# Gate and up of the second FFN by a seven-product (Strassen-Winograd) identity, with the down products of the previous tile set between them

## The chip, the cores and the metric

One core of one Trainium2 chip runs the whole program in one launch. The metric is the device time in microseconds (us), the median of several executions.

## The reference, cut to what matters

One layer of a diffusion backbone over 1024 latent tokens of width 1024 and 256 context tokens. Only its last part is touched by the change:

```python
def swiglu(h, w_gu, w_down):
    gate, up = jnp.split(h @ w_gu, 2, axis=-1)
    return (jax.nn.silu(gate) * up) @ w_down
...
x = x + mx[5] * mix_x
x = x + 0.5 * mx[8] * swiglu(modulate(x, g_ffn2[l], mx[6], mx[7]), w_gu2[l], w_down2[l])
...
return rmsnorm(x, g_final)
```

Here `h` is 1024 x 1024, `w_gu` 1024 x 5632 and `w_down` 2816 x 1024, all float32.

## The kernel before

Every matrix product is made of three matmuls (`mm3`, lines 622 to 626): both operands are split into a rounded high part H and a rest L, and H·H, H·L and L·H are summed in one PSUM bank. A split (`split`, line 618) is a copy on ScalarE (line 619, it writes H) and a subtraction (line 62, it writes L) on GpSimd (POOL) or VectorE (DVE).

`mix_out_ffn2` is the last part of the program. Its first half, the output projection, goes over eight token tiles `t` of 128 tokens. `part(t, ...)` issues 48 matmuls into two banks named `wo`; `evac(t)` scales them, adds them to the residual stream `acc[t]`, and takes the sum of squares; `xnorm(t)` writes the normalised tile `xn`. For odd t, `z_T` (line 1600) transposes the next two tiles of `z` after k = 4 of `part(t)`; DVE scales them just before. The first tile of gate and up weights is loaded (`w2r`) and split here, at t = 2 to 5. At t = 6 `trans(0, k)` transposes and modulates tokens 0 to 511 into `hT[0]` (H and L, eight k tiles).

The second half calls `ffn` (line 656). The hidden width is cut into NF = 22 tiles `f` of 128. For one f, gate is [128 hidden, 512 tokens], a sum over eight k tiles, for two token blocks b; up is the same. That is 4 results x 8 k x 3 = 96 matmuls of 512 columns, in banks `gu`. The down product adds, for each of eight token tiles and two halves of the 1024 outputs, one `mm3` into a bank `dn`, which DVE adds to `acc`: 16 x 3 = 48 matmuls for one f. The order on TensorE (PE) is gate(f), all down tiles of f-1, up(f). For f = 0 the transposes of tokens 512 to 1023 are set between the matmuls of block 1. The last two f (20 and 21, `joint`) are summed in one bank per down tile, and each finished token tile is normalised and stored while the next is computed (`final`). Weights stream in by DMA, 512 KB a piece, into four `raw` buffers, and are split on arrival; the down weight is first multiplied by the gate row `g8` on DVE (`raw<-raw,g`).

Each engine works through its own list in order, and waits on semaphores where the next instruction's data or buffer is not ready.

Of the kernel before, what the change touches and what calls it, by code (L numbers as in the profile page):

```python
# [15 lines left out]
MUL, ADD, SUB, POW = ALU.mult, ALU.add, ALU.subtract, ALU.pow  # L16

D = 1024
KT = 8
NX = 8  # L20
# [3 lines left out]
NF = FF // 128  # L24
# [23 lines left out]
class Kernel:  # L48
    def __init__(self, tc, a, out, dbg=None):
        self.tc, self.nc, self.a, self.out = tc, tc.nc, a, out  # L50
        self.dbg = dbg or {}
# [566 lines left out]
    def split(self, raw, H, L, eng=None):  # L618
        self.nc.scalar.activation(out=H, in_=raw, func=AF.Copy)  # L619
        self.tt(L, raw, H.bitcast(F32), SUB, eng)  # L620
# [953 lines left out]
    def mix_out_ffn2(self, sbig):  # L1574
        nc, a, acc = self.nc, self.a, self.acc
        B2 = [(0, 4), (4, 4)]
        with ExitStack() as st:
            hA = self.pool(st, "hT2a")
            hT = [tuple(hA.tile([128, KT, 512], F32R, name=f"h{x}0") for x in "HL")]
            w2 = self.pool(st, "w2")  # L1580
            P = {"w": w2}
            xp = self.pool(st, "xn", bufs=4)
            with ExitStack() as s1:
                tp = self.pool(s1, "wo", bufs=2)
                sm = self.pool(s1, "wos")
# [61 lines left out]
                def evac(t):  # L1647
                    ps = PS.pop(t)
                    for half in range(2):
                        cs = slice(half * 512, half * 512 + 512)  # L1650
                        self.stt(mo[:, cs], ps[half], ra[:, t:t + 1], g5[:, cs], MUL, MUL)
                    self.tt(acc[t], acc[t], mo, ADD, nc.gpsimd)
                    R[t] = self.rstd(self.sumsq(acc[t], mo, "n"), D, "n")

                def xnorm(t):
# [20 lines left out]
                def trans(b, kt, tag="gu"):  # L1676
                    self.modT([XN[i] for i in range(4 * b, 4 * b + 4)], kt, 2, 0, tag, hT[b], hf)
# [16 lines left out]
                    if t % 2 and k == 4 and t < NX - 1:  # L1694
                        z_T(t // 2 + 1)

                pre0 = {}
                for t in range(2, NX):
                    if t in (2, 4):
                        which = t // 2 - 1  # L1700
                        wr = sm.tile([128, D], F32, tag="wor", name="w2r")
                        nc.sync.dma_start(wr, a["w_gu2"][0, which].rearrange("p k f -> p (k f)"))
                    if t in (3, 5):
                        pre0[0, which] = [tuple(w2.tile([128, 1024], F32R, tag=f"w{x}{which}", name=f"w{x}{which}")
                                                for x in "HL")]
                        self.split(wr, *pre0[0, which][0], nc.gpsimd)
                    part(t, range(8), lambda k: pre(t, k))
                    if t % 2:
                        nxt(t // 2 + 1)
                    evac(t)  # L1710
                    for i in {2: (1,), 3: (2,), 4: (3,), 6: (4, 5), 7: (6, 7)}.get(t, ()):
                        xnorm(i)
                sbig.close()
                hB = self.pool(st, "hT2b", side="right")
                hT.append(tuple(hB.tile([128, KT, 512], F32R, name=f"h{x}1") for x in "HL"))
            P["act"] = P["wd"] = self.pool(st, "act2", bufs=2)
            P["raw"] = self.pool(st, "raw2", bufs=4)
            P["sg"], P["nsg"] = self.pool(st, "sg2"), 3
            fin = self.pool(st, "fin2")
            g8 = fin.tile([128, D], F32, name="g8")  # L1720
            gf = fin.tile([128, D], F32, name="gf")
            self.gate_bc(g8, (8, 0))
            nc.sync.dma_start(gf, a["g_final"].to_broadcast([128, D]))
            P["gates"] = [(g8, P["act"])]
            out = self.out.rearrange("(j s) d -> j s d", s=NX)

            def hook(b):
                todo = list(range(KT if b else 0))

                def pre(kt):  # L1730
                    while todo and todo[0] <= kt + 2:
                        trans(1, todo.pop(0), "dn")
                return pre

            down = self.ffn(B2, hT, a["w_gu2"], a["w_down2"], acc, P, hook, preload=pre0, keep=True, joint=True)
            S = {}

            def post(t, cs, p):
                self.tt(acc[t][:, cs], p, acc[t][:, cs], ADD)

            def final(t):
                R = self.rstd(S.pop(t), D, "n")
                for q in range(2 if t == NX - 1 else 1):
                    cs = slice(q * 512, q * 512 + 512) if t == NX - 1 else slice(0, D)
                    self.stt(J[t][:, cs], acc[t][:, cs], R, gf[:, cs], MUL, MUL)
                    nc.sync.dma_start(out[:, t, cs], J[t][:, cs])

            J = {}
            for t in range(NX):
                down([t], post)  # L1750
                J[t] = xp.tile([128, D], F32, tag="xn", name="j")
                S[t] = self.sumsq(acc[t], J[t], "n")
                if t:
                    final(t - 1)
            final(NX - 1)


def layouts(inp):
# [76 lines left out]
```

## Time and profile before

| | |
|---|---|
| median of 3 runs | 2529.99 us (2527.86 to 2538.18) |
| the profiled execution, its own time | 2531.55 us |
| its span | 2529.8 us, 31981 instructions |
| PE busy | 2417.6 us (96%), 12100 matmuls |
| DVE, ACT, POOL busy | 1454.1 (57%), 819.8 (32%), 1041.7 (41%) |

The span runs from the first to the last instruction; 1.75 us of the execution's own time lie around it. A busy share is the part of the span in which the engine ran an instruction. Matmuls are pipelined, so that one takes 0.39 us from its start to its end, but the next one starts earlier.

### The profile page before, as it was taken

How to read it: one execution, taken by the hardware profiler on the slowest of the kernel's cores; microseconds unless marked ns; L12 is line 12 of the kernel's file. 1: busy time of each engine (PE TensorE's matmuls, PEld its weight loads, DVE VectorE, ACT ScalarE, POOL GpSimd, SP SyncE). 2: the span in 40 equal slices, each digit the busy share in tenths (PEclk: the TensorE clock that was granted, in tenths of full speed). 3: DMA queues.
4: the chain of work that ended last, by engine and by line, in shares of the span. 5: the costliest groups of instructions: out<-in, count | busy, mean ns of one | idle time of the engine just before them, and what ended most of it. 6: DMA issues, size and time to landing. Idle time of an engine off the chain costs nothing. (4 is left out here: it accounts for less than half of the span.)

```text
span 2529.8 us, 31981 instructions
## 1 busy us (share of the span) xinstructions
PE 2417.6 (96%) x12100; PEld 1999.2 (79%) x12100; DVE 1454.1 (57%) x2468; ACT 819.8 (32%) x1572; POOL 1041.7 (41%) x949
## 2 busy tenths in 40 slices
PE   7999999999999998988999999999999999999998
PEld 3788888888888887887787777777788888888886
DVE  3666466966554627647788888862344444444443
ACT  4311211121111111633777777762411111111112
POOL 2422321254344334525676666755433322332222
PEclk9999999999999999999999999999999999999999
DMA  7232352122222232415000000123211111111111
GB/s 282 77 108 93 125 175 84 47 63 65 76 84 76 64 97 95 138 46 184 23 17 4 14 14 25 40 91 99 75 51 50 43 50 50 51 50 42 50 42 67
DMA packets 83544, 185.14 MB, mean 73 GB/s; under 512 B 22199, under 2 KB 41911, under 8 KB 82366
## 3 DMA queue, kind: packets, MB, share of 16 engines
q1 hardware_dynamic: 59990, 163.93, 19.4%
q10 hardware_dynamic: 23400, 19.16, 2.6%
q8 instruction: 95, 1.56, 0.2%
q14 instruction: 59, 0.48, 0.1%
HBM read 155.52 MB, written 27.54 MB: 72 GB/s over the span
## 5 line engine op out<-in xcount | busy, mean ns | idle before, releaser
L62 POOL TENSOR_TENSOR wL<-raw,wH 128x1024 fp32r<-128x1024 f32 x130 | 316.3, 2437 | 767.6 <-ACT wH L619 749.6
L62 DVE TENSOR_TENSOR acc<-dn,acc 128x512 f32<-128x512 f32 x540 | 366.9, 690 | 338.8 <-PE dn L626 338.6
L624 PE MATMUL gu<-big,wH 128*128 128x512 f32 (+1 forms) x1056 | 379.7, 360 | 4.9 <-ACT wH L619 2.3
L626 PE MATMUL gu<-big,wL 128*128 128x512 f32 (+1 forms) x1056 | 374.8, 355 | 4.6 <-POOL wL L62 4.6
L625 PE MATMUL gu<-big,wH 128*128 128x512 f32 (+1 forms) x1056 | 374.7, 355 | 1.8 <-POOL big L62 1.8
L624 PE MATMUL dn<-wH,aH 128*128 128x512 f32 x792 | 313.5, 396 | 10.7 <-DVE acc L62 5.5
L625 PE MATMUL dn<-wL,aH 128*128 128x512 f32 x792 | 310.5, 392 | 1.7 <-POOL wL L62 1.7
L626 PE MATMUL dn<-wH,aL 128*128 128x512 f32 x792 | 310.4, 392 | 1.1 <-POOL aL L62 1.1
L62 DVE TENSOR_TENSOR sg<-gu,sg 128x512 f32<-128x512 f32 (+1 forms) x110 | 69.9, 636 | 376.7 <-PE gu L626 348.8
L625 PE MATMUL gu<-hL,wH 128*128 128x512 f32 x704 | 274.6, 390 | 4.2 <-POOL hL L62 3.0
L619 ACT ACTIVATE wH<-raw 128x1024 fp32r<-128x1024 f32 x130 | 136.3, 1056 | 436.2 <-DVE raw L62 227.7
L624 PE MATMUL gu<-hH,wH 128*128 128x512 f32 x704 | 274.6, 390 | 0.0
L626 PE MATMUL gu<-hH,wL 128*128 128x512 f32 x704 | 274.0, 389 | 0.0
L62 POOL TENSOR_TENSOR aL<-sg,aH 128x512 fp32r<-128x512 f32 (+1 forms) x110 | 139.0, 1264 | 296.9 <-ACT aH L619 296.5
L624 PEld LDWEIGHTS gu<-big,wH 128*128 128x128 f32 x1056 | 200.0, 189 | 37.3 <-issue 3.3
L626 PEld LDWEIGHTS gu<-big,wL 128*128 128x128 f32 x1056 | 199.9, 189 | 34.4 <-POOL wL L62 6.4
L625 PEld LDWEIGHTS gu<-big,wH 128*128 128x128 f32 x1056 | 200.1, 190 | 31.1 <-POOL big L62 2.2
L619 ACT ACTIVATE aH<-sg 128x512 fp32r<-128x512 f32 (+1 forms) x110 | 64.5, 588 | 473.4 <-DVE sg L62 458.9
L62 DVE TENSOR_TENSOR ptL<-pt,ptH 128x512 fp32r<-128x512 f32 x240 | 162.7, 685 | 52.2 <-ACT ptH L1427 51.6
L624 PEld LDWEIGHTS dn<-wH,aH 128*128 128x128 f32 x792 | 150.1, 190 | 43.7 <-DVE acc L62 6.7
L625 PEld LDWEIGHTS dn<-wL,aH 128*128 128x128 f32 x792 | 150.1, 190 | 33.7 <-POOL wL L62 2.3
L626 PEld LDWEIGHTS dn<-wH,aL 128*128 128x128 f32 x792 | 149.8, 189 | 33.2 <-POOL aL L62 1.6
(318 smaller groups left out, 4635.2 us busy)
## 6 DMA issues: line engine op xcount, KB each, us to landing
raw<-in_w_gu SPq DMA_DIRECT2D x86, 512.0 KB, 3.4
wmr<-in_w_mod SPq DMA_DIRECT2D x56, 512.0 KB, 4.0
raw<-in_w_down SPq DMA_DIRECT2D x44, 512.0 KB, 4.7
row<-d_s SPq DMA_DIRECT2D x16, 576.0 KB, 3.7
wm<-in_w_mod SPq DMA_DIRECT2D x8, 1024.0 KB, 9.4
d_s<-T ACTq DMA_DIRECT2D x32, 160.0 KB, 2.7
ck<-d_s SPq DMA_DIRECT2D x16, 320.0 KB, 3.8
acc<-in_x SPq DMA_DIRECT2D x8, 512.0 KB, 9.1
```

Source lines behind the costliest of these rows:

```text
L62: (eng or self.nc.vector).tensor_tensor(out=out, in0=a, in1=b, op=op)
L619: self.nc.scalar.activation(out=H, in_=raw, func=AF.Copy)
L624: mm(out, lhsT=AH, rhs=BH, start=start, stop=False)
L625: mm(out, lhsT=AH, rhs=BL, start=False, stop=False)
L626: mm(out, lhsT=AL, rhs=BH, start=False, stop=stop)
```

## The change

With A11, A12 = the two k halves of the gate weight, A21, A22 = those of the up weight, B11, B21 = the k halves of tokens 0 to 511, and B12, B22 = those of tokens 512 to 1023, gate and up for both blocks are a 2 x 2 block product, which takes eight half products. The change computes it with seven:

- sums of weights, for each f: S1 = A21 + A22, S2 = S1 - A11, S3 = A11 - A21, S4 = A12 - S2 (DVE, `Products.add`; for f = 0 `Products.sums`, which uses one tile `s` for S1, S2 and S4 in turn);
- sums of tokens, once: T1 = B12 - B11, T2 = B22 - T1, T3 = B22 - B12, T4 = B21 - T2 (`part` in `ffn2`). B11 and B21 exist only as H and L; PE adds them up with a rounded identity `one` into banks `rc`;
- seven products of four k tiles each, 12 matmuls a product: A11·B11, S2·T2, S3·T3, S1·T1, A12·B21, A22·T4, S4·B22. DVE and ACT combine the banks in four 512-wide pieces of `acc[8]` and `acc[9]` (`P1`, `U2`, `U3`, `C22`), and the two activations of one f come out one after the other.

Each operand is split into H and L on ACT and POOL, seven splits of 128 x 512 for one f. The down products of f-1 are issued two token tiles at a time between the products of f. The down tiles of f = 20 are no longer joined to those of f = 21. There is one raw buffer for each weight half and one for the down weight. The last `acc` add of the output projection goes from POOL to DVE.

```diff
-                    self.tt(acc[t], acc[t], mo, ADD, nc.gpsimd)
+                    self.tt(acc[t], acc[t], mo, ADD, None if t == NX - 1 else nc.gpsimd)
...
                 for t in range(2, NX):
-                    if t in (2, 4):
-                        which = t // 2 - 1
-                        wr = sm.tile([128, D], F32, tag="wor", name="w2r")
-                        nc.sync.dma_start(wr, a["w_gu2"][0, which].rearrange("p k f -> p (k f)"))
-                    if t in (3, 5):
...
-                        self.split(wr, *pre0[0, which][0], nc.gpsimd)
+                    if t == 2:
+                        wr = [sm.tile([128, D], F32, tag="wor", name="w2r"), raw1.tile([128, D], F32, tag="r", name="w2r")]
+                        for which in range(2):
+                            nc.sync.dma_start(wr[which], a["w_gu2"][0, which].rearrange("p k f -> p (k f)"))
+                    if t == 3:
+                        prep = ops.sums(*wr, xp.tile([128, 512], F32, tag="hf", name="s", bufs=2))
+                    if t in (3, 4, 5):
+                        next(prep, None)
                     part(t, range(8), lambda k: pre(t, k))
...
-            down = self.ffn(B2, hT, a["w_gu2"], a["w_down2"], acc, P, hook, preload=pre0, keep=True, joint=True)
...
+    def ffn2(self, st, sx, h0, ops, raw1, xp, XN):
...
+        def part(k, tt, one):
+            f, r = [], []
+            for kt, pool, tag in ((k, xp, "hf"), (k + 4, tt, "b22")):
+                t = self.bank("dn", "tp")
+                for i in range(4):
+                    nc.tensor.transpose(t[:, i * 128:(i + 1) * 128], XN[4 + i][:, kt * 128:(kt + 1) * 128], self.ident)
+                x = pool.tile([128, 512], F32, tag=tag, name=tag, bufs=2)
+                nc.scalar.activation(out=x, in_=t, func=AF.Identity, scale=av[:, kt:kt + 1], bias=bv[:, kt:kt + 1])
+                f.append(x)
+            for x in ("B11", "B21"):
+                p = self.bank("dn", "rc")
+                for i in range(2):
+                    nc.tensor.matmul(p, lhsT=one, rhs=B[x][i][:, k, :], start=(i == 0), stop=(i == 1))
+                r.append(p)
...
+            self.tt(t1, b12, r[0], SUB)
+            self.split(t1, *g("T1"), nc.gpsimd)
+            self.tt(t2, b22, t1, SUB)
+            self.split(t2, *g("T2"), nc.gpsimd)
+            self.tt(t4, r[1], t2, SUB)
+            self.tt(t3, b22, b12, SUB)
+            self.split(t4, *g("T4"))
+            self.split(t3, *g("T3"), nc.gpsimd)
+            self.split(b22, *g("B22"), nc.gpsimd)
...
+                sx.close()
...
+                self.gate_bc(g8, (8, 0))
+                load_gu(1, (1,))
+                fetch_wd(0)
+                ops.add(*W[1], temps)
+                for x in ("S2", "S3", "S1"):
+                    ops.split(x)
+                load_wd(0)
+            else:
+                more = f + 1 < NF
+                fetch_wd(f)
+                nc.scalar.copy(P1, whole("A11"))
...
+                self.tt(U2, whole("S2"), P1, ADD)
...
+                down(f - 1, (0, 1))
+                self.tt(U3, whole("S3"), U2, ADD)
+                if more:
+                    ops.add(*W[f + 1], temps)
+                down(f - 1, (2, 3))
+                p = whole("S1")
+                self.tt(C22, p, U3, ADD)
+                self.tt(U2, p, U2, ADD)
+                for x in ("A11", "S2", "S3", "S1") if more else ():
+                    ops.split(x)
+                if f > 1:
+                    self.tt(P1, whole("A12"), P1, ADD)
+                    nc.scalar.activation(out=P1, in_=P1, func=AF.Silu)
+                down(f - 1, (4, 5))
+                p4 = whole("A22")
+            self.tt(U3, p4, U3, ADD)
+            self.tt(P1, P1, U3, MUL)
+            act[f] = [split_act(0, P1)]
+            if f:
+                down(f - 1, (6, 7))
+                load_wd(f)
+            self.tt(U2, whole("S4"), U2, ADD)
+            nc.scalar.activation(out=U2, in_=U2, func=AF.Silu)
+            self.tt(C22, U2, C22, MUL)
+            act[f].append(split_act(1, C22))
+            if f + 1 < NF:
+                for x in ("A12", "A22", "S4")[f == 0:]:
+                    ops.split(x)
+            load_gu(f + 2)
...
+            R, J = self.rstd(S.pop(t), D, "n"), acc[8 + t % 2]
...
+    def sums(self, g, u, t):
...
+        k.tt(t, a21, s["A22"], ADD)
+        s["S1"] = s["S2"] = s["S4"] = t
+        self.split("S1")
+        k.tt(t, t, s["A11"], SUB)
+        self.split("S2")
+        yield
```

`load_wd(f)` multiplies the down weight by `g8` on DVE and splits it on ACT and POOL, as before. `whole(x)` issues one product of 12 matmuls.

Three places show how instructions moved. First, DVE at t = 3 of the output projection, where `z<-z,ia` is the scaling ahead of `z_T` and `s` and `w2r` are the tile for the sums and the raw weight:

```order
 L66 TENSOR_SCALAR rv<-ss 128x1
 L66 TENSOR_SCALAR xn<-acc,rr 128x1024
+L62 TENSOR_TENSOR s<-w2r 128x512
+L62 TENSOR_TENSOR s<-s,w2r 128x512
 L66 TENSOR_SCALAR z<-z,ia 128x256 x2
 L62 TENSOR_TENSOR big<-zt,big 128x256 x2
```

S1 and S2 now stand ahead of the scaling of z, and the second of them overwrites the tile that the first wrote.

Second, DVE in the first step (f = 0) of the changed kernel, one of four quarters k; `hf` and `b_...` are b12 and b22, `rc` a PSUM bank, `t_...` T1, T2, T4 and T3 in this order:

```order
L62 TENSOR_TENSOR t_16534<-hf,rc 128x512
L62 TENSOR_TENSOR t_16535<-b_16526,t_16534 128x512
L62 TENSOR_TENSOR t_16537<-rc,t_16535 128x512
L62 TENSOR_TENSOR t_16536<-b_16526,hf 128x512
L62 TENSOR_TENSOR T4L<-t_16537,T4H 128x512
```

Before, DVE had one subtraction `hL<-hf,hH` for every second k tile there; now it has five operations for each pair of k tiles, three of them (T2, T3 and T4L) with both inputs in SBUF.

Third, DVE in one f of the steady part, before and then changed (`S_...` and `A_...` are banks of products, `rw` a raw weight, `wdr` the raw down weight):

```order
L62 TENSOR_TENSOR acc<-dn,acc 128x512 x16
L62 TENSOR_TENSOR raw<-raw,g_16405 128x1024
L62 TENSOR_TENSOR sg<-gu,sg 128x512 x2
```

```order
L62 TENSOR_TENSOR s<-rw,s 128x512
L62 TENSOR_TENSOR acc<-dn,acc 128x512 x4
L62 TENSOR_TENSOR acc<-S_17325,acc 128x512 x2
L62 TENSOR_TENSOR acc<-A_17356,acc 128x512
L62 TENSOR_TENSOR acc<-dn,acc 128x512 x4
L62 TENSOR_TENSOR acc<-A_17391,acc 128x512
L62 TENSOR_TENSOR acc<-acc 128x512
L62 TENSOR_TENSOR acc<-dn,acc 128x512 x4
L62 TENSOR_TENSOR wdr<-wdr,g_16692 128x1024
L62 TENSOR_TENSOR acc<-S_17435,acc 128x512
```

The multiplication of the down weight by `g8` used to stand ahead of up(f), with the 96 matmuls of up(f) and gate(f+1) between it and the down tiles that need it; now it stands behind the adds of the last two down tiles of f-1, and only the 36 matmuls of S4·B22, A11·B11 and S2·T2 come before the next down tiles.

## Rows read from the trace of the kernel before

**Rows 1.** The page, part 4: the chain that ended last, by line.

```profile
PE gu L625 6%; PE gu L626 6%; PE gu L624 6%; PE dn L626 3%; PE dn L625 3%; PE dn L624 3%; DVE acc L62 0%; DVE j L69 0%; POOL rr L62 0%; DVEq L1828 0%; POOLq L1828 0%; DVE rv L66 0%; POOLq L62 0%
```

**Rows 2.** Windows: us, busy of PE, PEld, DVE, ACT, POOL, PE clock, DMA share, GB/s.

```profile
1900.00:2000.00 100.00, 100.00 (x443) 82.81 (x442) 42.30 (x61) 16.28 (x22) 31.10 (x16) 1.00 0.14 48
```

**Rows 3.** Timeline of PE: start, us, operation; second FFN's first matmul, two in between, first last-step down.

```profile
1790.73 0.39 PE L624 MATMUL gu<-hH,wH 128*128 128x512 f32 x1
...
1849.93 0.39 PE L624 MATMUL gu<-hH,wH 128*128 128x512 f32 x1
...
1862.17 0.39 PE L624 MATMUL gu<-hH,wH 128*128 128x512 f32 x1
...
2496.61 0.39 PE L624 MATMUL dn<-wH,aH 128*128 128x512 f32 x1
```

**Rows 4.** Groups by line and shape, 1850 to 2490 us: busy us, mean ns, idle before.

```profile
L62 DVE TENSOR_TENSOR acc<-dn,acc 128x512 f32<-128x512 f32 x304 | 206.9, 692 | 204.8 <-PE dn L626 204.8
L62 DVE TENSOR_TENSOR raw<-raw,g 128x1024 f32<-128x1024 f32 x20 | 24.3, 1217 | 0.0
L62 POOL TENSOR_TENSOR wL<-raw,wH 128x1024 fp32r<-128x1024 f32 x59 | 141.5, 2398 | 333.6 <-ACT wH L619 333.6
L62 POOL TENSOR_TENSOR aL<-sg,aH 128x512 fp32r<-128x512 f32 x40 | 51.7, 1294 | 114.7 <-ACT aH L619 114.7
L619 ACT ACTIVATE wH<-raw 128x1024 fp32r<-128x1024 f32 x59 | 62.1, 1052 | 211.5 <-DVE raw L62 211.5
L619 ACT ACTIVATE aH<-sg 128x512 fp32r<-128x512 f32 x40 | 25.3, 632 | 162.8 <-DVE sg L62 162.8
```

**Rows 5.** Timeline of DVE and POOL: subtractions with two SBUF inputs, adds from PSUM.

```profile
1772.37 0.69 DVE L62 TENSOR_TENSOR hL<-hf,hH 128x512 fp32r<-128x512 f32 x1 [1.18 <-ACT hf L614]
...
1776.57 1.30 POOL L62 TENSOR_TENSOR hL<-hf,hH 128x512 fp32r<-128x512 f32 x1 [1.35 <-DVE hf L66]
1776.62 1.80 DVE L62 TENSOR_TENSOR hL<-hf,hH 128x512 fp32r<-128x512 f32 x1
...
2062.97 10.21 DVE L62 TENSOR_TENSOR acc<-dn,acc 128x512 f32<-128x512 f32 x15
...
2063.35 2.41 POOL L62 TENSOR_TENSOR wL<-raw,wH 128x1024 fp32r<-128x1024 f32 x1 [7.47 <-ACT wH L619]
```

**Rows 6.** Timeline of PE in the first step (f = 0): first and last wait, one transpose.

```profile
1804.37 0.50 PE L625 MATMUL gu<-hL,wH 128*128 128x512 f32 x1 [0.56 <-DVE hL L62]
...
1807.13 0.60 PE L607 MATMUL tp<-ident,xn 128*128 128x128 f32 x4
...
1815.99 0.50 PE L625 MATMUL gu<-hL,wH 128*128 128x512 f32 x1 [0.95 <-POOL hL L62]
```

**Rows 7.** Timeline of DVE and PE around `z_T` at t = 3.

```profile
1737.05 0.61 DVE L66 TENSOR_SCALAR z<-z,ia 128x256 f32<-128x256 f32 x2
...
1738.42 0.60 PE L1600 MATMUL zt<-ident,z 128*128 128x128 f32 x4
```

**Rows 8.** DMA issues, 1790 to 1800 us, then out from 1800 us: KB, us to landing.

```profile
raw<-in_w_gu SPq DMA_DIRECT2D x3, 512.0 KB, 7.0
gf<-in_g_final SPq DMA_DIRECT2D x1, 512.0 KB, 5.1
...
out<-j SPq DMA_DIRECT2D x7, 512.0 KB, 2.6
```

**Rows 9.** Timeline of DVE in the last step: first add, first two norms.

```profile
2498.17 0.69 DVE L62 TENSOR_TENSOR acc<-dn,acc 128x512 f32<-128x512 f32 x1 [0.60 <-PE dn L626]
...
2502.86 0.14 DVE L66 TENSOR_SCALAR rv<-ss 128x1 f32<-128x1 f32 x1
...
2506.07 0.14 DVE L66 TENSOR_SCALAR rv<-ss 128x1 f32<-128x1 f32 x1
```

**Rows 10.** Windows of PE alone, an idle stretch: us, busy, PE clock, DMA share, GB/s.

```profile
990.00:1000.00 10.00, 3.26 (x22) 0.83 0.11 34
1000.00:1010.00 10.00, 8.63 (x26) 0.66 0.12 36
```

More of the change, by code (lines that the diff above doesn't have):

```diff
@@ L1580, in mix_out_ffn2 @@
             w2 = self.pool(st, "w2")
-            P = {"w": w2}
-            xp = self.pool(st, "xn", bufs=4)
+            raw1 = self.pool(st, "raw1")
+            sx = ExitStack()
+            xp = self.pool(sx, "xn", bufs=4)
+            ops = Products(self, w2)
             with ExitStack() as s1:
@@ L1695, in pre @@
                         z_T(t // 2 + 1)
-                pre0 = {}
                 for t in range(2, NX):
-                    if t in (2, 4):
-                        which = t // 2 - 1
-                        wr = sm.tile([128, D], F32, tag="wor", name="w2r")
-                        nc.sync.dma_start(wr, a["w_gu2"][0, which].rearrange("p k f -> p (k f)"))
-                    if t in (3, 5):
-                        pre0[0, which] = [tuple(w2.tile([128, 1024], F32R, tag=f"w{x}{which}", name=f"w{x}{which}")
-                                                for x in "HL")]
-                        self.split(wr, *pre0[0, which][0], nc.gpsimd)
+                    if t == 2:
[6 more added lines that the diff above has]
+                        next(prep, None)
                     part(t, range(8), lambda k: pre(t, k))
@@ L1713, in mix_out_ffn2 @@
                 sbig.close()
[L1714 to L1733, printed above, removed]
-            down = self.ffn(B2, hT, a["w_gu2"], a["w_down2"], acc, P, hook, preload=pre0, keep=True, joint=True)
@@ L1736, in mix_out_ffn2 @@
[L1736 to L1748, printed above, removed]
@@ new lines, with __init__, __getitem__, add @@
+class Products:
+    def __init__(self, k, pool):
+        self.k, self.pool, self.src, self.t = k, pool, {}, {}
+    def __getitem__(self, x):
+        return self.t[x]
+    def add(self, g, u, temp):
+        self.gate(g)
+        k, s = self.k, self.src
+        a21, s["A22"] = u[:, 0:512], u[:, 512:1024]
+        s["S1"] = temp()
+        k.tt(s["S1"], a21, s["A22"], ADD)
+        s["S2"] = temp()
+        k.tt(s["S2"], s["S1"], s["A11"], SUB)
+        s["S3"] = a21
+        k.tt(a21, s["A11"], a21, SUB)
+        s["S4"] = temp()
+        k.tt(s["S4"], s["A12"], s["S2"], SUB)
+    def gate(self, g):
+        self.src["A11"], self.src["A12"] = g[:, 0:512], g[:, 512:1024]
+    def split(self, x):
+        self.t[x] = tuple(self.pool.tile([128, 512], F32R, tag=x + y, name=x + y) for y in "HL")
+        self.k.split(self.src.pop(x), *self.t[x], self.k.nc.gpsimd)
+    def sums(self, g, u, t):
+        s, k = self.src, self.k
+        half = lambda x, i: x[:, i * 512:(i + 1) * 512]
+        s["A11"], s["A12"], a21, s["A22"] = half(g, 0), half(g, 1), half(u, 0), half(u, 1)
+        k.tt(t, a21, s["A22"], ADD)
[4 more added lines that the diff above has]
+        yield
+        k.tt(a21, s["A11"], a21, SUB)
+        s["S3"] = a21
+        self.split("S3")
+        self.split("A11")
+        yield
+        k.tt(t, s["A12"], t, SUB)
+        for x in ("S4", "A12", "A22"):
+            self.split(x)
```

107 lines of the change are left out of this document (100 added, 7 removed).

## The prediction

> **What bounds the kernel now.** I began with the chain that ended last [rows 1]: its largest lines are matmuls of `gu` and `dn`, and everything else has a share that rounds to zero. The windows say the same of the steady part of the second FFN [rows 2]: PE is busy for all of 100 us at full clock, DVE for 42, ACT for 16 and POOL for 31. So a matmul that is taken out there shortens the program, if the work that feeds the others stays hidden. The price of a matmul is its distance to the next, not its 0.39 us: between two starts of L624 [rows 3] lie 54 matmuls in 12.24 us, 0.2267 us each. From the first gate matmul at 1790.73 to the first down matmul of the last step at 2496.61 [rows 3] are 705.9 us. The 22 x 96 + 20 x 48 = 3072 matmuls in it cost 696.3. Eight groups of four transposes take about 0.45 each (0.36 to the next matmul [rows 6], which then starts a little late), 3.6 together. The remaining 6.0 are waits, all in the first step, between the first and the last wait of [rows 6]. What follows, 33.2 us to the end of the span, is set by DVE and not by PE: a token tile takes 3.2 us there (2502.86 to 2506.07 [rows 9]), while its 12 matmuls need 2.7.
>
> **Matmuls.** Gate and up of one f cost 7 x 12 = 84 matmuls instead of 96. 22 x 12 = 264 fewer at 0.2267 are **-59.8 us**, all on the path. Against this stand 16 matmuls `rc`, **+3.6**. The transposes stay eight groups.
>
> **Steady steps (f = 1 to 21).** One step is 132 matmuls, 29.9 us instead of 32.6. For one f, DVE has 16 adds and nine combinations at 0.69, four sums of weights at 0.69 or less and one product at 1.22 [rows 4], some 21 us. POOL has nine subtractions at 1.29 and one at 2.40, 14 us. ACT has nine copies at 0.63, one at 1.05, and a copy and two activations of about 0.6, 9 us. All fit under 29.9. The question is the closest chain. After the last down tile of f-1 (2.7 us before the end of S4·B22) DVE still has the adds, which end about 1.4 us before that end. Then come the product with `g8` 1.22, H 1.05 and L 2.40 [rows 4] and some 0.2 for the handovers: L of the down weight is there 3.4 us after the end of S4·B22. PE asks for it after A11·B11 and S2·T2 and one more matmul, 5.7 us after. That leaves 2.3 us. The DMA of the next up weight can start only when POOL has split A22, about 8.6 us after, and is needed at 11.7 for the sums; even if it is late, PE wants nothing from those sums until the next f. So I cost the steady steps at **0**; if the cover of 2.3 us is used up, every microsecond beyond it costs 21.
>
> **Output projection, t = 3.** S1 (0.69), its H (0.63) and L (1.29) and S2 (0.69) come ahead of the scaling of z on DVE, because S2 overwrites the tile that POOL is still reading for S1. With 0.3 for handovers z is 3.6 us later. Before, it was ready at 1737.66 and its transposes began at 1738.42 [rows 7], 0.76 of slack. PE stands still for **+2.8 us**. It could be 0, if the steps in between were free, or 4. At t = 5 one sum of 0.69 eats that slack and no more. The other splits there are on ACT and POOL, ahead of the splits of the attention output for the next tiles; they come at most 1.5 us later, and are needed later than that. The last `acc` add goes from a POOL operation to a DVE one of about 1.2 us, which gives back about 1.2 us ahead of the transposes; it only shortens a wait that I count next.
>
> **First step (f = 0).** A11·B11 and A12·B21 need nothing new, 5.4 us, in which the last normalised tile is finished; PE waits perhaps 0.5 us for it. Then four quarters follow, each with four POOL subtractions (T1, T2, T3, B22), 4 x 1.29 = 5.2 us, and PE must have T3 of a quarter for its products. The rows show something that raises this price. A DVE subtraction with two SBUF inputs took 0.69 us alone. Started just behind a POOL one, at 1776.62 against 1776.57, it took 1.80 and ended 0.55 after POOL did [rows 5]. DVE adds that read one input from PSUM kept their pace of 0.68 (10.21 for 15) while POOL ran beside them [rows 5]. So DVE and POOL take turns, and three of the five DVE operations of a quarter (T2, T3, T4L) have two SBUF inputs: 5.2 + 3 x 0.69 = 7.2 us a quarter. The Trainium skill has this as a rule (SBUF — State Buffer, section "Who interferes with whom"): a DVE instruction with two SBUF inputs contends with a GpSimd instruction that reads SBUF, and the loser waits for the whole of the other. The rows agree with it, and it speaks against this change.
>
> From the last normalised tile on: 3.4 us until the first POOL subtraction (transposes 0.9, activation 0.8, T1 0.7, H 0.6, handovers), three quarters of 7.2, the last one up to T3 (3 x 1.29 + 2 x 0.69 = 5.3), eight matmuls 1.8 and S4·B22 2.7: 34.8 us. PE works in it for 3.6 (transposes) + 3.6 (`rc`) + 60 x 0.2267 = 13.6, 20.8 us. Waits: 14.0 + 0.5, against 6.0 before, **+8.5 us**. By POOL alone it would be 27.3 us and the waits 7.0, +1.0. I take 8.5, since the taking of turns is in the rows.
>
> **Into f = 1.** The new buffers lie where the first step's tiles were, so the up weight of f = 1 and the first down weight can be fetched only when POOL has finished with B22, some 31.6 us after the last normalised tile. DMAs issued together landed after 5.1 and 7.0 us [rows 8]. The sums are then done by 38.8; POOL has three splits at 1.29, the down weight 2.40 and the first activation 1.29, 7.6 us, and yields to DVE for 1.22 and 0.69: 48.3. PE gets to the matmul that needs that activation at 34.8 + 3 x 2.72 + 0.45 = 43.4. **+4.9 us**. Without turns and with a quicker DMA, the nearest row being the 2.6 of an output tile alone [rows 8], about 2; with the DMAs landing one behind the other, 9.
>
> **Last step.** The 48 down matmuls of f = 20 were under DVE's pace in the last step, and now run before the last product: **+10.9**. Down tile 0 waits for the down weight (3.4 us), but DVE then has its adds back to back, so that the first norm comes about 0.7 later than before. The output tile is kept in `acc[8]` or `acc[9]` in turn, so the last sum of squares waits for the store of two tiles earlier (2.6 [rows 8]); 0.8 more. **+1.5 us** (0 to 5).
>
> **Sum.** -59.8 + 3.6 + 0 + 2.8 + 8.5 + 4.9 + 10.9 + 1.5 = -27.6. The profiled execution took 2531.55, so 2503.9; it stands 1.6 above the median of the runs, and I forecast **2502 us**.
>
> **Rivals.**
> *Quick first step.* POOL and DVE don't stand in each other's way as much: 1.0 in place of 8.5, 2.6 in place of 4.9: 2492. For it: a waiting engine can use the other's pauses. Against it: four POOL operations follow each other there without a pause.
> *Slow first step.* The quarters don't overlap, because each hands work from PE to ACT, DVE, ACT and POOL and back: 10 us a quarter instead of 7.2, +11, 2513. The clock could add to it: after an idle stretch of almost 7 us it fell to 0.66 for 10 us, some of the time at the 1.2 GHz level [rows 10], which costs PE up to 3.4 us. Against it: T1 and the activations of the next quarter need nothing of the quarter before.
> *A wait in every step.* Slower than before. The down weight's product with `g8` waits on DVE behind the adds and the combinations, and its L part comes after S2·T2 has ended. Up to 2.3 us of lateness are free, each one more costs 21. It decides at 2.3 + 27.6/21 = 3.6 us; if the chain were 6 us late, 21 x 3.7 = 78, the time would be 2580. For it: the cover was 96 matmuls and is 36. Against it: all its operations are in [rows 4] with little spread, and POOL is free at that time.
> *The change doesn't do what it says.* PE's list would be as long as before. The order of instructions speaks against it: the products have 12 matmuls each and there are seven.
>
> **How the numbers follow.** Forecast (2496 to 2510): 0.55. Quick first step: 0.18. Slow first step: 0.13, of which 0.04 end within 0.5%. A wait in every step: 0.12, of which 0.05 are slower and 0.07 cancel about all of the gain. No shorter list: 0.02. A difference below 0.5%, 12.6 us, is about what a measurement of this kernel can't tell from none; faster means under 2517.3. Faster: 0.55 + 0.18 + 0.09 = 0.82; same: 0.04 + 0.07 + 0.02 = 0.13; slower: 0.05. The range must reach to most of both first-step cases: 2490 to 2518.
>
> **What would show it.** In the changed profile, the starts of a steady f should lie 29.9 us apart with PE always busy; a group of waits of `dn` for `wdL` on POOL would show the third rival. PE should stand still about 2.8 us at the transposes of z at t = 3, some 14 us in all in the first step, most of it released by POOL's T2L and T3L, and 5 us at the first down tiles. DVE operations with two SBUF inputs should last over 1 us on average in the first step. The tail from the last S4·B22 to the end should be about 34.7 us. The prediction is wrong if the steady step is not 29.9, or if the first step and the entry cost under 8 or over 25 us more than before.

## The result, and the profile after

The changed kernel takes **2504.04 us** (median of 4 runs, 2501.97 to 2508.66), the kernel before on the same chip 2531.12 (2527.86 to 2538.18): a ratio of 0.9892, 95% interval 0.9866 to 0.9917. The forecast was 2502. The profiled execution took 2503.74 us with a span of 2501.9, against 2531.55 and 2529.8 before, 27.9 us of span less; the prediction's sum was -27.6.

The steady part first. The window that stands in [rows 2] for the kernel before, now for the changed kernel (us, busy of PE, PEld, DVE, ACT, POOL, PE clock, DMA share, GB/s):

```profile
1900.00:2000.00 100.00, 100.00 (x443) 82.81 (x442) 67.20 (x97) 27.23 (x45) 48.82 (x36) 1.00 0.19 63
```

DVE, ACT and POOL have over half as much again to do as before, and PE still never waits. The timeline of PE in the changed kernel gives the borders of the parts, as [rows 3], [rows 6] and [rows 7] did (start, us, operation, in brackets the wait before it):

```profile
1741.89 0.81 PE L1602 MATMUL zt<-ident,z 128*128 128x128 f32 x4 [2.20 <-DVE z L66]
...
1794.46 0.39 PE L624 MATMUL A<-hH,A11H 128*128 128x512 f32 x1
...
1833.03 0.39 PE L626 MATMUL S<-B22H,S4L 128*128 128x512 f32 x1
...
1847.75 0.39 PE L624 MATMUL S<-T3H,S3H 128*128 128x512 f32 x1
...
2464.96 0.39 PE L626 MATMUL S<-B22H,S4L 128*128 128x512 f32 x1
2466.18 0.50 PE L624 MATMUL dn<-wdH,aH 128*128 128x512 f32 x1 [0.84 <-ACT wdH L619]
2468.61 0.80 PE L625 MATMUL dn<-wdL,aH 128*128 128x512 f32 x1 [1.93 <-POOL wdL L62]
```

From the first S3·T3 of f = 1 at 1847.75 to the end of the last S4·B22 (its last matmul starts at 2464.96) are 617.44 us, and the 2724 matmuls in it need 2724 x 0.22667 = 617.45. The four parts below take their borders from the same places in every kernel: the **first step** (first gate matmul to end of S4·B22, 38.8 us here), the **entry** (to the first S3·T3 of f = 1, 14.5), the **steady part** (617.4) and the **tail** (to the end of the span, 36.7).

DVE ahead of the transposes of z, as in [rows 7] (timeline; S2, then the scaling of z):

```profile
1740.88 0.69 DVE L62 TENSOR_TENSOR s<-s,w2r 128x512 f32<-128x512 f32 x1 [2.04 <-POOL S1L L62]
1741.49 0.61 DVE L66 TENSOR_SCALAR z<-z,ia 128x256 f32<-128x256 f32 x2
```

S2 waits 2.04 us for POOL to read S1; z itself takes 0.61 us, as before.

The groups of DVE and POOL in the first step, 1798 to 1828 us, which answer to [rows 5] (busy us, mean ns, idle before):

```profile
L62 POOL TENSOR_TENSOR T2L<-t,T2H 128x512 fp32r<-128x512 f32 x4 | 6.9, 1718 | 0.0
L62 POOL TENSOR_TENSOR B22L<-b,B22H 128x512 fp32r<-128x512 f32 x4 | 6.6, 1647 | 0.0
L62 POOL TENSOR_TENSOR T1L<-t,T1H 128x512 fp32r<-128x512 f32 x4 | 6.5, 1613 | 1.7 <-ACT T1H L619 1.7
L62 POOL TENSOR_TENSOR T3L<-t,T3H 128x512 fp32r<-128x512 f32 x4 | 5.6, 1396 | 0.0
L62 DVE TENSOR_TENSOR T4L<-t,T4H 128x512 fp32r<-128x512 f32 x4 | 7.1, 1764 | 0.0
L62 DVE TENSOR_TENSOR t<-b,hf 128x512 f32<-128x512 f32 x4 | 4.1, 1026 | 0.0
...
L62 DVE TENSOR_TENSOR t<-rc,t 128x512 f32<-128x512 f32 x4 | 2.8, 691 | 0.4
```

DVE operations with two SBUF inputs last 1.03 and 1.76 us, those with one in PSUM (`rc`) 0.69. POOL doesn't pause from T1 to B22: 1.61 + 1.72 + 1.40 + 1.65 = 6.4 us a quarter. These means hide two lengths: in the timeline, 11 of POOL's 16 subtractions took 1.71 to 1.82 us and five 1.27 to 1.30, and 11 DVE operations with two SBUF inputs ran beside them. So one turn of DVE costs POOL about 0.43 us. The clock of PE in the same step, as in [rows 10] (columns as in the first window):

```profile
1805.00:1810.00 5.00, 3.05 (x10) 1.86 (x10) 4.50 (x6) 4.13 (x7) 5.00 (x4) 0.91 0.00 2
1810.00:1815.00 5.00, 5.00 (x21) 3.79 (x20) 3.65 (x5) 3.68 (x6) 5.00 (x5) 0.75 0.01 3
...
1825.00:1830.00 5.00, 3.55 (x9) 2.71 (x10) 1.66 (x3) 1.72 (x2) 3.87 (x3) 0.66 0.27 63
```

The entry: when the transfers are issued, and when DVE can begin with the sums of the up weight (timelines of the DMA queue and of DVE).

```profile
1827.66 0.32 SPq L803 DMA_DIRECT2D g<-d_gate  x1
1828.03 0.42 SPq L1771 DMA_DIRECT2D rw<-in_w_gu  x1
1828.90 0.33 SPq L1776 DMA_DIRECT2D wdr<-in_w_down  x1
```

```profile
1833.56 0.69 DVE L62 TENSOR_TENSOR s<-rw 128x512 f32<-128x512 f32 x1 [2.16 <-DMA rw<-in_w_gu]
```

And DVE in the last step, as in [rows 9]:

```profile
2469.87 0.69 DVE L62 TENSOR_TENSOR acc<-dn,acc 128x512 f32<-128x512 f32 x1 [0.77 <-PE dn L626]
2471.15 0.69 DVE L62 TENSOR_TENSOR acc<-dn,acc 128x512 f32<-128x512 f32 x1 [0.59 <-PE dn L626]
...
2473.71 0.69 DVE L62 TENSOR_TENSOR acc<-dn,acc 128x512 f32<-128x512 f32 x1 [0.59 <-PE dn L626]
2474.32 0.14 DVE L66 TENSOR_SCALAR rv<-ss 128x1 f32<-128x1 f32 x1
...
2496.50 0.15 DVE L66 TENSOR_SCALAR rv<-ss 128x1 f32<-128x1 f32 x1 [0.65 <-ACT acc L588]
```

The first four adds come 1.28 us apart, the time of three matmuls at the half of the clock (0.427 each); at full clock it would be 0.69, DVE's own pace. The clock in that stretch (columns as in the first window):

```profile
2470.00:2475.00 5.00, 5.00 (x14) 3.84 (x13) 2.69 (x5) 1.66 (x3) 1.65 (x2) 0.53 0.25 90
```

### The profile page after: what moved, and what is told of

Same layout as the page of the kernel before. It is cut to its first block, busy times and chain, and to the rows that moved or that the text cites. A ratio compares the mean times of both kernels' runs of the same rounds, so it can differ in the third digit from the quotient of the medians.

```text
span 2501.9 us, 32006 instructions
## 1 busy us (share of the span) xinstructions
PE 2376.1 (95%) x11852; PEld 1961.6 (78%) x11852; DVE 1649.2 (66%) x2739; ACT 886.3 (35%) x1721; POOL 1154.6 (46%) x1070
## 4 chain that ended last, share of the span: by engine, by line
PE 36%; DVE 8%; ACT 4%; issue 2%; POOL 2%; DMA 1%; SPq 0%; ACTq 0%; DVEq 0%; POOLq 0%
PE dn L626 3%; PE dn L625 3%; PE dn L624 3%; PE S L624 3%; PE S L626 3%; PE S L625 3%; DVE ptL L62 2%; PE A L624 2%; PE A L626 2%; PE A L625 2%; DVE mx L1398 2%; PE pt L1424 2%; ACT ptH L1427 1%; PE scA L624 1%; DVE mx L62 1%
## 5 line engine op out<-in xcount | busy, mean ns | idle before, releaser
L62 POOL TENSOR_TENSOR wL<-raw,wH 128x1024 fp32r<-128x1024 f32 x66 | 162.5, 2469 | 408.9 <-ACT wH L619 378.5
L624 PE MATMUL dn<-wH,aH 128*128 128x512 f32 x440 | 175.8, 400 | 10.1 <-ACT aH L619 5.3
L625 PE MATMUL dn<-wL,aH 128*128 128x512 f32 x440 | 172.8, 393 | 1.7 <-POOL wL L62 1.7
L626 PE MATMUL dn<-wH,aL 128*128 128x512 f32 x440 | 173.0, 393 | 1.1 <-POOL aL L62 1.1
L1427 ACT CAST ptH<-pt 128x512 fp32r<-128x512 f32 x240 | 138.4, 586 | 46.5 <-PE pt L1424 41.6
L624 PE MATMUL dn<-wdH,aH 128*128 128x512 f32 x352 | 138.4, 393 | 5.6 <-DVE acc L62 4.8
L619 ACT ACTIVATE wH<-raw 128x1024 fp32r<-128x1024 f32 x66 | 68.9, 1058 | 208.3 <-PE dn L626 71.4
L619 ACT ACTIVATE aH<-sg 128x512 fp32r<-128x512 f32 (+1 forms) x66 | 36.7, 559 | 298.8 <-DVE sg L62 288.6
L625 PE MATMUL dn<-wdL,aH 128*128 128x512 f32 x352 | 138.5, 393 | 3.2 <-POOL wdL L62 3.2
L626 PE MATMUL dn<-wdH,aL 128*128 128x512 f32 x352 | 138.3, 393 | 1.2 <-POOL aL L62 1.2
L62 DVE TENSOR_TENSOR acc<-S,acc 128x512 f32<-128x512 f32 x110 | 73.7, 686 | 97.8 <-ACT acc L1843 58.0
```

What stands on the lines that cost most here:

```text
L62: (eng or self.nc.vector).tensor_tensor(out=out, in0=a, in1=b, op=op)
L624: mm(out, lhsT=AH, rhs=BH, start=start, stop=False)
L625: mm(out, lhsT=AH, rhs=BL, start=False, stop=False)
L626: mm(out, lhsT=AL, rhs=BH, start=False, stop=stop)
L1427: nc.scalar.copy(H, p)
```

## The experiments

The theory is the sum of the prediction: PE's list sets the time, and the 32 us that are missing from 59.8 go into extra matmuls and waits, each with a name, ahead of the steady part and behind it. The rivals are named with each run. Single runs scatter by some 7 us ahead of the second FFN (first gate matmul at 1793.0 to 1800.2 us where nothing ahead of it differs from the changed kernel), so they are compared part by part.

| us | first step | entry | steady | tail | span | time |
|---|---|---|---|---|---|---|
| changed kernel | 38.8 | 14.5 | 617.4 | 36.7 | 2501.9 | 2504.0 |
| S2 in a tile of its own | 40.2 | 14.4 | 617.8 | 36.1 | 2500.2 | |
| operands from PSUM | 33.0 | 17.1 | 618.3 | 35.6 | 2497.3 | |
| T2's L part on DVE | 41.0 | 15.3 | 617.5 | 36.0 | 2503.9 | |
| `rc` twice | 38.9 | 13.8 | 617.4 | 36.1 | 2501.9 | |
| buffers in another order | 39.1 | 12.2 | 617.4 | 34.5 | 2496.2 | |
| down weight late, one operation | 40.2 | 16.7 | 618.3 | 37.3 | 2512.7 | |
| down weight late, two operations | 39.1 | 19.7 | 640.7 | 40.4 | 2535.3 | 2538.0 |
| joint last step | 39.0 | 14.3 | 606.6 | 34.0 | 2491.4 | 2492.7 |
| B22 and T4 in PSUM | 32.9 | 12.3 | 617.4 | 36.1 | 2494.4 | |
| all four together | 34.1 | 12.3 | 606.6 | 34.1 | 2479.1 | 2484.3 |
| changed kernel again | 38.9 | 14.2 | 617.4 | 35.9 | 2500.5 | 2506.1 |

**S2 in a tile of its own.**

```diff
-        s["S1"] = s["S2"] = s["S4"] = t
+        s["S1"], s["S2"], s["S4"] = t, t2, t2
...
-        k.tt(t, t, s["A11"], SUB)
+        k.tt(t2, t, s["A11"], SUB)
```

> S1 and S2 of the up weight of f = 0 get tiles of their own; nothing else changes. Theory (DVE's subtraction for S2 has to wait until ACT and POOL have read S1, and the scaling of z stands behind it): z is scaled about 2 us sooner, PE's wait at the transposes of z for t = 3 falls from 2.20 us to 0.2 to 0.7, and the first gate matmul comes 1.5 to 2.0 us earlier against the start of the output projection. Rival (DVE is slow there because it and POOL take turns, whoever owns the tile): the wait stays above 1.5 us.

Timelines of DVE and POOL, then PE, of this kernel:

```profile
1737.78 1.63 DVE L66 TENSOR_SCALAR z<-z,ia 128x256 f32<-128x256 f32 x2
...
1737.88 1.37 POOL L62 TENSOR_TENSOR S1L<-s,S1H 128x512 fp32r<-128x512 f32 x1 [0.94 <-ACT S1H L619]
```

```profile
1738.19 0.33 PE L1602 MATMUL zt<-ident,z 128*128 128x128 f32 x1 [0.20 <-DVE z L66]
1739.47 0.55 PE L1602 MATMUL zt<-ident,z 128*128 128x128 f32 x3 [0.95 <-DVE z L66]
```

The wait falls from 2.20 to 1.15 us, and from the `wo` matmul that waits for the first evacuated tile (1721.75 in the changed kernel, 1720.65 before) to the first gate matmul it takes 71.7 us instead of 72.7 (70.1 before the change). The wait lies between the theory's 0.2 to 0.7 and the rival's 1.5: S2 no longer waits, but the scaling of z now runs into POOL's S1, and its two halves take 1.63 us instead of 0.61 [rows 7]. The gain up to the first gate matmul is 1.0 and not 1.5 to 2. In this run it doesn't last: to the first S3·T3 of f = 1 it takes 126.3 us from the same `wo` matmul, 126.0 in the changed kernel. Counted from the first gate matmul, POOL's subtractions of the first step stand at the same places to 0.02 us. But from the last T3 to the end of the step PE's clock is 0.65 over 7.0 us (0.82 over 5.6 in the changed kernel), and it falls again in the entry, where PE's matmuls are 0.43 us apart from 1843.8 to 1846.4.

**Operands from PSUM.** T2, T3 and T4's L part are formed with an `rc` bank in place of an SBUF operand, so that they hold other values.

```diff
-            self.tt(t2, b22, t1, SUB)
+            self.tt(t2, b22, r[0], SUB)
...
-            self.tt(t3, b22, b12, SUB)
+            self.tt(t3, b22, r[1], SUB)
...
```

> In the first step T2 and T3 are formed from an operand in PSUM (the copy of B11 or B21) in place of one in SBUF, and the L part of T4 is taken against the PSUM copy: every DVE operation there has one PSUM input. Left as they should be are only T1 and B22; T2, T3 and the L part of T4 hold other values, so the output is another. Number and length of the operations stay. Theory (DVE and POOL take turns when DVE reads two SBUF inputs): POOL's four subtractions fall from 1.40 to 1.72 to about 1.29 us, DVE's from 1.0 to 1.76 to 0.69 us, a quarter takes 5.3 us and not 6.3, and the 38.8 us from the first gate matmul to the end of S4 x B22 become about 34.5. Rival one (the handovers between PE, ACT, DVE and POOL set the quarter): durations fall but the 38.8 stays within 1 us. Rival two (the durations come from something else): POOL stays at 1.6 and the 38.8 stays.

Groups of POOL and DVE of this kernel, 1798 to 1828 us:

```profile
L62 POOL TENSOR_TENSOR T3L<-t,T3H 128x512 fp32r<-128x512 f32 x4 | 5.2, 1299 | 0.0
...
L62 POOL TENSOR_TENSOR T2L<-t,T2H 128x512 fp32r<-128x512 f32 x4 | 5.1, 1286 | 0.0
...
L62 DVE TENSOR_TENSOR T4L<-rc,T4H 128x512 fp32r<-128x512 f32 x4 | 2.8, 692 | 0.4
```

The same operations in the same number, and T2 falls from 1.72 to 1.29 us, T4's L part from 1.76 to 0.69. The quarter shrinks to 5.0 us, with POOL still never pausing, and the first step from 38.8 to 33.0 us (forecast 34.5). The inputs that T2 and T3 no longer read, T1 and b12, were ready anyway (T1 is the operation just ahead on DVE). So taking turns is shown, and so is that it lies on the path; 2.6 us of the 5.8 come back in the entry.

**T2's L part on DVE.**

```diff
-            self.split(t2, *g("T2"), nc.gpsimd)
+            self.split(t2, *g("T2"))
```

> In the first step the L part of T2 is done by DVE and not by POOL, four operations in all. Theory (POOL's queue sets the quarter): three subtractions of about 1.65 us, a quarter of 5.0 to 5.3 us in place of 6.3, the 38.8 us become about 35. Theory of strict turns: the sum of a quarter goes from 4 x 1.29 + 3 x 0.69 = 7.2 to 3 x 1.29 + 4 x 0.69 = 6.6, a twelfth less; 38.8 becomes about 37. Rival (DVE, now with six operations of which four are stretched to 1.76, becomes the bound): 8.4 us a quarter and about 46 in all.

Timelines of POOL and of DVE of this kernel, first quarter:

```profile
1807.47 1.27 POOL L62 TENSOR_TENSOR T3L<-t,T3H 128x512 fp32r<-128x512 f32 x1 [2.49 <-ACT T3H L619]
```

```profile
1804.38 1.14 DVE L62 TENSOR_TENSOR T2L<-t,T2H 128x512 fp32r<-128x512 f32 x1 [0.69 <-ACT T2H L619]
```

No theory held: 41.0 us. DVE isn't full and POOL idles. T2's L part stands on DVE ahead of T4 and T3 and waits there for ACT's H; T3 with its H comes that much later, and POOL waits 2.49 us for it in each quarter. The quarter (T1 of POOL starts at 1810.10 and 1816.81) is 6.7 us, and neither engine is full in it: DVE waits another 1.15 us for ACT's next `hf`. So handovers set it; which of them, no run here shows. Moving work off the busy engine gained nothing, because it was put into the middle of another engine's queue.

**`rc` twice.**

```diff
-                for i in range(2):
+                for i in (0, 1, 0, 1):
```

> The matmuls that copy B11 and B21 to PSUM in the first step are done twice over, 16 more of them, 3.6 us of work at full clock that falls into stretches in which PE waits; values are the same. Theory (PE's half clock from 1808.98 to 1811.82 and from 1826.45 to 1829.6 follows the waits, and it lies on the path): PE waits less in one piece, the granted clock is at least 0.9 from 1805 to 1830, and the step takes 36 to 39 us although it has 3.6 us more work. Rival (the half clock costs nothing, since PE waits for POOL anyway): the clock may rise, the step takes 38.5 to 40. Rival two (PE sets the quarter): 38.8 + 3.6 = 42.

Windows of this kernel (columns as above):

```profile
1805.00:1810.00 5.00, 3.49 (x15) 2.20 (x14) 4.57 (x5) 4.06 (x8) 5.00 (x4) 1.00 0.00 2
1810.00:1815.00 5.00, 4.87 (x26) 3.81 (x25) 4.45 (x5) 4.38 (x7) 5.00 (x4) 1.00 0.02 3
...
1825.00:1830.00 5.00, 2.51 (x7) 1.75 (x8) 2.01 (x3) 2.45 (x4) 4.64 (x4) 0.81 0.11 29
```

The clock stays at its full level up to 1825 and 3.6 us more of PE's work vanish in its waits, yet the step is not shorter, 38.9. That lies in the range of the theory and of its first rival; POOL decides between them. Its T2 operations start 6.9, 6.3 and 6.3 us apart, as in the changed kernel (6.8, 6.4, 6.3), so POOL's queue sets the quarter and PE's half clock early in the step costs nothing here. The dip at the end remains: from the end of the last T3's L part to the end of S4·B22 it takes 6.1 us here and 5.6 in the changed kernel, against 4.7 in the three runs whose clock is at 1.00 there (operands from PSUM, B22 and T4 in PSUM, all four together). So the dip is worth 0.9 us of the changed kernel's first step, and up to 2.3 in other runs (7.0 us with S2 in its own tile and in the run with the down weight late by one operation). Part of it is missing from the entry's wait afterwards: with S2 in its own tile the dip is 1.4 us longer than in the changed kernel, and PE then waits 0.44 us for the first down weight instead of 1.27.

**Buffers in another order.**

```diff
-                W["act"] = self.pool(st, "act2")
-                W["raw"] = self.pool(st, "raw2")
                 g8 = self.pool(st, "fin2").tile([128, D], F32, name="g8")
+                W["raw"] = self.pool(st, "raw2")
+                W["act"] = self.pool(st, "act2")
```

> The same buffers in another order: g8 and the raw weights of the steady steps lie where the normalised tiles of the first step were, and the split activations and down weights take the places that come free last. Theory (the entry into f = 1 costs 3.6 us because the transfers of g8, of the up weight and of the first down weight start only after POOL's last subtraction on B22): these transfers start 4 us or more sooner, the sums of the up weight begin by 1831 on the scale of the changed kernel (1833.56 there), and from the end of S4 x B22 to the first S3 matmul of f = 1 it takes 11 to 12.5 us in place of 14.5. Rival (the queues of DVE and POOL set it, not the transfers): the transfers come sooner and the 14.5 stays within 0.7.

Timeline of DVE of this kernel, at the entry and in the last step:

```profile
1830.04 0.68 DVE L62 TENSOR_TENSOR s<-rw 128x512 f32<-128x512 f32 x1
...
2465.91 2.78 DVE L62 TENSOR_TENSOR acc<-dn,acc 128x512 f32<-128x512 f32 x4 [0.29 <-PE dn L626]
2468.60 0.15 DVE L66 TENSOR_SCALAR rv<-ss 128x1 f32<-128x1 f32 x1
```

The transfers are issued 11 us sooner (`g` at 1816.32 instead of 1827.66). The sums follow the products without a wait for the transfer; they begin at 1831.5 on the scale of the changed kernel (forecast 1831), and the entry falls from 14.5 to 12.2 us: the theory. What is left is a wait of 0.98 us for POOL's split of the first activation. The tail gave something that wasn't asked for: the end of the last S4·B22 is at 2461.71 there, PE waits for the down weight as before, but the clock stays at 1.00, the four adds come back to back, and the first norm is 6.9 us behind that end; the tail is 34.5. The window (columns as above):

```profile
2465.00:2470.00 5.00, 4.87 (x21) 4.03 (x22) 4.04 (x7) 2.93 (x5) 1.93 (x3) 1.00 0.27 105
```

**Down weight late.** One or two more POOL operations ahead of the L part.

```diff
+            for _ in range(2):
+                self.tt(L, r, r, SUB, nc.gpsimd)
             self.split(r, H, L, nc.gpsimd)
```

> One more POOL subtraction of 128x1024 (2.4 us) ahead of the L part of each down weight, in all 22 steps; its result is overwritten. ACT makes the H part in the meantime (1.1 us), so L is late by about 1.3 us. Theory (a cover of 2.3 us in the steady step): nothing in f = 2 to 21, PE busy 100 of 100 us; 1.3 us each at the entry and in the last step, where the wait for L is already on the path: +2.6 us in all. Rival (no cover left): 21 x 1.3 = 27 us more, 2531.

> Two such POOL subtractions: L late by about 3.7 us. Theory (a cover of 2.3 us): 1.4 us over in each of the 20 steady steps, 28 us, and 3.7 each at the entry and in the last step: +35 us, about 2539, slower than the kernel before the change; PE waits for L of the down weight in every step. Rival one (no cover): 22 x 3.7 = 81, 2585. Rival two (POOL's work there is never on the path): +7 at most. If the clock falls with a wait in every step, more than +35.

Of the kernel with one, a window of the steady part; of the kernel with two, PE's waits from 1860 to 2480 us (sum, times, longest):

```profile
2000.00:2450.00 450.00, 450.00 (x1987) 372.71 (x1987) 296.17 (x450) 121.67 (x198) 245.38 (x166) 1.00 0.16 53
```

```profile
PE dn L625 <- POOL wdL L62: 16.4, 20, 0.8
```

With one operation PE is busy for 450 of 450 us; entry, start of the steady part and tail grow by 2.2, 0.9 and 0.6, together 3.7 against a forecast of 2.6. Another 7.1 of that run's 10.8 us of span lie where the edit isn't (5.7 ahead of the first gate matmul, 1.4 in the first step). With two the time is 2538.0 (8 runs), a ratio to the kernel before of 1.0024 (1.0013 to 1.0035): +34 against a forecast of +35. The tail took 3.7 more, the entry 5.3, and the steady part 23.3, or 1.16 a step instead of 1.4; that the sum is so close is in part luck.

How late L was, and how large the cover is, can be read off the timelines of PE and POOL: first the last matmul of S4·B22 (the product ends 0.23 us after its start), the L part and PE's first use of it in one steady step of the changed kernel, then that matmul and the L part in the kernel with two operations.

```profile
1986.24 0.39 PE L626 MATMUL S<-B22H,S4L 128*128 128x512 f32 x1
1987.49 2.40 POOL L62 TENSOR_TENSOR wdL<-wdr,wdH 128x1024 fp32r<-128x1024 f32 x1 [2.68 <-ACT wdH L619]
1992.13 0.39 PE L625 MATMUL dn<-wdL,aH 128*128 128x512 f32 x1
```

```profile
1997.67 0.39 PE L626 MATMUL S<-B22H,S4L 128*128 128x512 f32 x1
2002.11 2.38 POOL L62 TENSOR_TENSOR wdL<-wdr,wdH 128x1024 fp32r<-128x1024 f32 x1
```

In the changed kernel L is there 3.4 us after the end of S4·B22, as forecast, and PE takes it 2.24 us later. That is the cover; the prediction had 2.3. With two operations L is there 6.6 us after that end, 3.2 us later than before and not 3.7, so that 0.9 us lie beyond the cover. They cost 1.16 a step, of which 0.82 is the wait itself. What lies beyond the cover, 20 times, and the two ends take back more than the change gains.

**Joint last step.** The down tiles of f = 20 wait for f = 21; its weights and activations lie in the places of used-up sums. The core of it:

```diff
-                    self.mm3(p, aH[:, ts], aL[:, ts], wd[f][0][:, cs], wd[f][1][:, cs], True, True)
+                    for i in fs:
+                        aH, aL = act[i][t // 4]
+                        self.mm3(p, aH[:, ts], aL[:, ts], *wd[i][half], i == fs[0], i == fs[-1])
```

> As before the change, the down tiles of f = 20 are kept back and added up in PSUM with those of f = 21, 12 matmuls to a tile; weights and activations of f = 21 lie in the places of used-up weight sums, and the down weight is split before the last product. Theory (48 down matmuls went from under DVE's pace of 3.2 us a tile to the path, 10.9 us, and the wait for the down weight with the half clock behind it cost 3.5): the time falls by 10.9 to 14.4 us against the changed kernel, 2490 to 2493. Rival (without the down tiles between them the products of the last step run into their evacuations, or the tail gets slower by what it takes on): a fall of under 6 us.

2492.71 us (4 runs), ratio 0.9842 (0.9827 to 0.9856), 11.3 below the changed kernel, which ran on another chip (the kernel before took 2532.35 and 2531.12 us on the two). The steady part loses the 48 matmuls (617.4 to 606.6), and the tail is 34.0 although each tile has 12 matmuls again: they fit under DVE. The clock is full in it:

```profile
2460.00:2465.00 5.00, 5.00 (x23) 4.13 (x22) 2.77 (x6) 2.54 (x5) 1.84 (x2) 1.00 0.02 3
```

**B22 and T4 in PSUM**, where T2 and T3 keep their values and T3 moves ahead of T4; **all four together** (this, the joint last step, the buffers and S2's tile); and the changed kernel again beside them. The core of the first edit:

```diff
+                x = t if pool is tt else pool.tile([128, 512], F32, tag=tag, name=tag, bufs=2)
...
+            t4 = r[1]
...
-            self.split(b22, *g("B22"), nc.gpsimd)
+            self.split(b22, *g("B22"))
```

> All values as in the changed kernel, but in the first step B22 (after scale and shift) and T4 are written to PSUM by ACT and DVE in place of SBUF, so that every DVE operation there has one PSUM input; the L part of B22, which POOL can't read from PSUM, goes to DVE. POOL keeps three subtractions, T1, T2 and T3. Theory (taking turns is what makes the quarter 6.3 us): DVE's operations all take 0.69 us, POOL's 1.29, the 38.8 us of the step become 32 to 34, as when the operands were merely taken from PSUM (33.0); the entry into f = 1 may take back up to 2.6 us of it. Rival (fewer operations on POOL help nothing, since the handovers over ACT and DVE set the quarter, as when T2's L part went to DVE and the step took 41.0): 38 or more.

> Four edits together: down tiles of the last two f added up in PSUM, buffers of the steady steps in the other order, a tile of its own for S2, and B22 and T4 of the first step in PSUM. From the single runs: -11.3 (timed), -2.3 (entry), -1.0 (transposes of z) and -5 us (first step), of which the entry may take back up to 2.6 from the last: 2484 to 2488 us, 0.981 to 0.983 of the kernel before. If the edits stand in each other's way, 2489 to 2493, no better than the joint last step alone.

> The changed kernel once more, on the chip of the combination and in as many rounds, so that the two can be compared: 2502 to 2506 us. In the profile, the last step is 36 to 37 us if the half clock follows the wait for the down weight again, and about 34.5 if it doesn't, as in the run with the buffers in another order; the steady part is 617.4 us either way.

Groups of the kernel with B22 and T4 in PSUM alone, 1785 to 1828 us:

```profile
L62 POOL TENSOR_TENSOR T1L<-t,T1H 128x512 fp32r<-128x512 f32 x4 | 5.2, 1292 | 5.3 <-ACT T1H L619 5.3
...
L62 DVE TENSOR_TENSOR T4L<-rc,T4H 128x512 fp32r<-128x512 f32 x4 | 2.8, 692 | 2.7 <-ACT T4H L619 2.7
...
L62 DVE TENSOR_TENSOR B22L<-tp,B22H 128x512 fp32r<-128x512 f32 x4 | 2.7, 680 | 0.0
```

The step takes 32.9 us. POOL now pauses 1.2 us ahead of each further quarter until T1's H is there, so it no longer sets the quarter of 5.0 us by itself. The entry falls too, to 12.3, since the raw tile places come free sooner (the transfer of the up weight is issued at 1820.73, 1828.03 in the changed kernel). All four together take **2484.31 us** (4 runs, 2480.87 to 2486.50), ratio 0.9813 (0.9798 to 0.9828), against 2506.08 and 0.9905 (0.9888 to 0.9921) for the changed kernel beside it: faster than both kernels of this case. Its first step is 34.1 and not 32.9: PE's clock was at 0.50 from 1806 to 1808, and DVE waited 1.47 us for the `rc` matmuls of the third quarter. Once POOL no longer holds up the step, the half clock does cost time there. The changed kernel's tail was 35.9 this time, with the first norm 8.3 us behind the last S4·B22.

## Why the prediction was right

- **Matmuls, -59.8 and +3.6, and steady steps 0**: as predicted, to 0.1 us in 617.4. The rival of a wait in every step is ruled out for this kernel, and the cover that excludes it is measured (2.24 us, forecast 2.3).
- **Output projection, +2.8**: +2.6. PE waits 2.20 us for DVE's scaling of z, and the mechanism was right: z comes late because S2 waits 2.04 us on DVE for the tile that POOL still reads for S1. What the prediction didn't name is the next obstacle, which shows once S2 has its own tile: POOL then slows the scaling of z itself, 1.63 us instead of 0.61.
- **First step, +8.5**: mis-sized, measured +6.5 (38.8 - 26.3 = 12.5 us beyond PE's work against 6.0; 0.9 of it is PE's half clock at the end of the step). The step that failed is 5.2 + 3 x 0.69 = 7.2 us a quarter; the starts of T2 on POOL at 1805.18, 1812.02, 1818.37 and 1824.68 give 6.8, 6.4 and 6.3. DVE does lose its turn for as long as was thought (1.76 for T4's L part), but a turn costs POOL 0.43 us and not 0.69, 1.2 a quarter and not 2.1. From the first to the last of these starts three quarters took 19.5 us instead of 21.6. The quick rival's figure for a step without turns, 7.0 us of waits or 33.3 in all, is what came out once the turns were taken away, 33.0 and 32.9; only the first of these runs is the case it was worked out for, four POOL operations on end.
- The Trainium skill (SBUF — State Buffer, section "Who interferes with whom") says that a DVE instruction with two SBUF inputs contends with POOL's reads and that the loser is blocked for the whole of the other. The operands-from-PSUM run agrees with the first part: both engines are back at about 1.29 and 0.69 us. DVE's 1.76 us for T4's L part behind POOL agrees with the second; the 0.43 us that a turn costs POOL is less than the 0.69 that the DVE operation takes alone, which is what the prediction had put in for it.
- **Into f = 1, +4.9**: +3.6. The mechanism was right: with the transfers earlier, 2.3 of it go. The sizes along the chain held as well: from the end of POOL's last B22 (1827.60 + 1.28) to the end of the sums (1836.2) 7.3 us, forecast 7.2. The step that failed is where PE stood: the end of S4·B22 came 4.4 us behind that last B22 and not 3.2, as PE's clock was at 0.66 in between (1825 to 1830), so that 1.2 us of the wait were already counted in the first step.
- **Last step, +10.9 and +1.5**: the 48 matmuls cost 10.9, and the joint step gets them back. The 1.5 was really +3.5 in the first profile. What failed is "the first norm comes about 0.7 later": 6.9 us behind the last S4·B22 was expected. Eight profiles have the same wait there: seven show the first norm after 8.0 to 9.1 us, the eighth, whose clock stayed full, after 6.9, and from that norm to the end it takes 27.6 to 27.7 us in all of them (26.9 before the change; 0.8 more was forecast). So the excess is the time that PE spends at 1.2 GHz behind the wait for the down weight, which the prediction had weighed for the first step alone.
- The sum held because the errors cancel: -0.2 (z), -2.0, -1.3, +2.0, and +1.1 from ahead of the `wo` matmul that waits for the first evacuated tile, where nothing was changed. So 27.9 against 27.6 is in part luck; the single terms are off by up to 2 us.

## What to carry to other kernels

A cut in the bounding engine's list is worth its full price only where it runs steadily; price the first and the last step separately, since there the new preparation has no cover (here only 27.9 of 59.8 us were left, and four edits there gave back some 22). State the cover of the closest chain in microseconds and measure it by delaying that chain: a step repeated 20 times forgives 2.2 us here and then charges more than 20 for each. When work is moved to relieve an engine, put it where the receiving queue holds up nobody, or take away the reason for the contention (an operand in PSUM).

## What was not expected of the hardware

- A DVE operation with one SBUF input can also lose its turn to POOL: scaling of z 1.63 us beside POOL's S1 instead of 0.61. The same section of the Trainium skill counts `tensor_scalar` among the instructions that may take the shared port, which agrees.
- The half clock came after waits of 0.84 and 1.93 us that followed 617 us of uninterrupted work, and stayed away in one profile with the same waits (buffers in another order); why is open.
